# A load cut in two and a store held back: the sixth chunk of a streaming RMSNorm on one Trainium2 core

## The chip, the cores and the metric

One core of one Trainium2 chip runs the kernel. The metric is the device time of one execution in microseconds (us). The profiler takes one execution apart. Its span (first to last instruction) is about 1.8 us shorter than the measured time.

## The reference

```python
batch, seq, dim = 16, 1024, 512          # x: float32, 33.55 MB
rms = np.sqrt(np.mean(x ** 2, axis=-1, keepdims=True) + eps)
return np.maximum(x / rms * gamma, 0).astype(np.float32)
```

Every row of 512 numbers is read once and written once: 67.1 MB in all.

## The kernel before

The 16,384 rows are cut into 8 chunks of 4 MB, each with 16 rows on each of 128 partitions. SBUF holds six slots of a chunk. One queue, SyncE's (SP in the profile), carries loads and stores. ScalarE squares and sums, VectorE scales, multiplies by gamma and clips, both in place in the slot.

```python
K = 16                      # rows of a chunk on one partition
G = 8                       # rows of one step of ScalarE and VectorE
nchunks = rows // K         # 8
nslots = 6
per = K // G                # 2
...
loads = [(0, 0, G), (0, G, K - G)] + [(i, 0, K) for i in range(1, nchunks)]
...
def load(m):
    i, a, r = loads[m]
    nc.sync.dma_start(out=slot_ap(i)[:, a:a + r, :], in_=xv[i][:, a:a + r, :]
                      ).then_inc(sem_half if m == 0 else sem_slot[i % nslots], 16)
...
def store(i):
    nc.sync.dma_start(out=ov[i], in_=slot_ap(i)).then_inc(sem_slot[i % nslots], 16)
...
for m, (i, a, r) in enumerate(loads):
    if i < nslots:
        load(m)                                   # chunks 0 to 5 at once
nxt = nslots
for i in range(nchunks):
    nc.sync.wait_ge(done, per * (i + 1))          # VectorE is through with chunk i
    store(i)
    if i >= 1 and nxt < nchunks:
        nc.sync.wait_ge(sem_slot[nxt % nslots], 32)   # an old store has landed
        ...                                       # load chunk nxt into the freed slot
        nxt += 1
```

Chunks count from 0, so the sixth chunk is chunk 5. The order of the queue is: load 0 in two halves, loads 1 to 5, store 0, store 1, load 6, store 2, load 7, stores 3 to 7. The 16 DMA engines move a whole chunk as 8 packets of 32 KB each, a half chunk as 8 packets of 16 KB each. I call the transfers that are queued and not yet moved the ring; it runs dry when nothing is left in it. I call the change from a load to a store, or back, a turn. The first turn is the one from load 5 to store 0.

## Time and profile before

| what | value |
|---|---|
| time, median (range, 6 runs) | 162.84 us (162.69 to 162.93) |
| span of the profiled run | 160.9 us |
| DMA engines busy, main queue | 97.6% |
| VectorE busy, ScalarE busy | 78%, 54% |
| bytes moved, mean rate | 67.1 MB, 417 GB/s |

How to read it: all bytes go through the 16 DMA engines, which are hardly ever idle. The compute engines have breaks. The span can shrink only where the DMA engines are idle or run below their usual rate. The prediction shows the lines.

### The profile page before, as it was taken

How to read it: one execution, taken by the hardware profiler on the slowest of the kernel's cores; microseconds unless marked ns; L12 is line 12 of the kernel's file. 1: busy time of each engine (PE TensorE's matmuls, PEld its weight loads, DVE VectorE, ACT ScalarE, POOL GpSimd, SP SyncE). 2: the span in 40 equal slices, each digit the busy share in tenths (PEclk: the TensorE clock that was granted, in tenths of full speed). 3: DMA queues.
4: the chain of work that ended last, by engine and by line, in shares of the span. 5: the costliest groups of instructions: out<-in, count | busy, mean ns of one | idle time of the engine just before them, and what ended most of it. 6: DMA issues, size and time to landing. Idle time of an engine off the chain costs nothing. (4 is left out here: it accounts for less than half of the span.)

```text
span 160.9 us, 1006 instructions
## 1 busy us (share of the span) xinstructions
DVE 126.0 (78%) x164; ACT 86.3 (54%) x273; POOL 0.2 (0%) x4
## 2 busy tenths in 40 slices
DVE  1103989898989899999999999999999999994000
ACT  3088929889988988988900198503994000000000
POOL 0000000000000000000000000000000000000000
DMA  5999999999999998999999999999999999999993
GB/s 155 434 432 415 521 391 391 513 399 391 489 424 391 481 432 367 415 391 489 424 391 489 424 391 448 464 391 440 456 407 432 456 415 424 464 415 424 464 407 138
DMA packets 2456, 67.12 MB, mean 417 GB/s; under 512 B 276, under 2 KB 276, under 8 KB 280
## 3 DMA queue, kind: packets, MB, share of 16 engines
q1 hardware_dynamic: 2448, 67.11, 97.6%
q10 hardware_dynamic: 8, 0.01, 0.0%
HBM read 33.56 MB, written 33.55 MB: 417 GB/s over the span
## 5 line engine op out<-in xcount | busy, mean ns | idle before, releaser
L124 ACT ACTIVATE junk<-slots 128x512 f32 x128 | 74.5, 582 | 30.6 <-ACTq L120 30.3
L148 DVE SCALAR_TENSOR_TENSOR slots<-slots,rstd,gamma_sb 128x512 f32 x128 | 86.2, 747 | 4.8 <-DVEq L145 4.8
L155 DVE TENSOR_SCALAR slots<-slots x16 | 36.7, 2294 | 2.4 <-DVEq L154 0.2
L124 ACT ACTIVATION_READ_ACCUMULATOR junk<-slots x128 | 23.9, 187 | 0.0
L142 DVE RECIPROCAL rstd<-rms x16 | 3.1, 196 | 6.3 <-DVEq L138 6.3
L131 ACT ACTIVATE rms<-ss,eps_sb x16 | 4.8, 301 | 3.0 <-ACTq L130 3.0
L135 DVE LOAD_MASK_SELECT gamma_sb<-gseed x1 | 0.0, 14 | 5.8 <-DMA gseed<-in_gamma_dram 5.8
L116 ACT ACT_TABLE_LOAD x1 | 1.3, 1283 | 2.8 <-issue 2.8
L109 DVE MEMSET gseed<- 128x512 f32 x1 | 0.5, 485 | 1.1 <-SPq L90 1.1
L135 DVE STREAM_SHUFFLE gamma_sb<-gseed 128x512 f32<-128x512 f32 x1 | 0.7, 715 | 0.0
L180 POOL MEMSET const-bfloat16-1.0<- 128x1 bf16 x1 | 0.1, 103 | 0.0
L180 POOL MEMSET const-uint8-127<- 128x1 uint8 x1 | 0.1, 102 | 0.0
L180 POOL MEMSET const-float32-0.0<- 128x1 f32 x1 | 0.1, 100 | 0.2 <-issue 0.2
L180 POOL MEMSET const-float32-1.0<- 128x1 f32 x1 | 0.1, 99 | 0.0
L110 DVE MEMSET eps_sb<- 128x1 f32 x1 | 0.1, 59 | 0.0
## 6 DMA issues: line engine op xcount, KB each, us to landing
out_dram<-slots SPq DMA_DIRECT2D x8, 4096.0 KB, 31.3
slots<-in_x_dram SPq DMA_DIRECT2D x7, 4096.0 KB, 30.3
slots<-in_x_dram SPq DMA_DIRECT2D x2, 2048.0 KB, 9.6
gseed<-in_gamma_dram ACTq DMA_DIRECT2D x1, 8.0 KB
```

Of the source, the lines that this page charges most:

```text
L109: nc.vector.memset(gseed, 0.0).then_inc(sem_z, 1)
L110: nc.vector.memset(eps_sb, eps).then_inc(sem_z, 1)
L116: nc.scalar.preload_act_table(ACTF.Sqrt)
L124: a = nc.scalar.activation(out=junk[:, j, :], in_=slots[:, bass.ds(base + j * d, d)], func=ACTF.Square, accum_out=ss[:, bass.ds(col + j, 1)])
L131: nc.scalar.activation(out=rms[:, bass.ds(col, G)], in_=ss[:, bass.ds(col, G)], func=ACTF.Sqrt, bias=eps_sb, scale=inv_d).then_inc(sq, 1)
L135: nc.vector.stream_shuffle(gamma_sb, gseed, [0] * 32)
L142: nc.vector.reciprocal(out=rstd[:, bass.ds(col, G)], in_=rms[:, bass.ds(col, G)]).then_inc(sv, 1)
L148: r = nc.vector.scalar_tensor_tensor(out=row, in0=row, scalar=rstd[:, bass.ds(col + j, 1)], in1=gamma_sb, op0=ALU.mult, op1=ALU.mult)
L155: nc.vector.tensor_scalar_max(out=blk, in0=blk, scalar1=0.0).then_inc(done, 1)
L180: nc = _bacc.Bacc("TRN2", target_bir_lowering=False, num_devices=1)
```

## The change

The intent: the last of the initial loads comes in two pieces, so that the first store can be queued at a chosen moment, when the first piece has landed, and not stand in the queue behind three loads for 30 us.

```diff
-    loads = [(0, 0, G), (0, G, K - G)] + [(i, 0, K) for i in range(1, nchunks)]
+    loads = [(i, a, r) for i in range(nchunks)
+             for a, r in (((0, G), (G, K - G)) if i in (0, nslots - 1) else ((0, K),))]
+    sem_half2 = tc.alloc_semaphore("half2")
...
+    def piece_sem(m):
+        i, a, r = loads[m]
+        if a + r < K:
+            return sem_half if i == 0 else sem_half2
+        return sem_slot[i % nslots]
...
-                          ).then_inc(sem_half if m == 0 else sem_slot[i % nslots], 16)
+                          ).then_inc(piece_sem(m), 16)
...
         for i in range(nchunks):
             nc.sync.wait_ge(done, per * (i + 1))
+            if i == 0:
+                nc.sync.wait_ge(sem_half2, 16)
             store(i)
```

The waits for a landed load are changed to match (cut here).

More of the change, by code (lines that the diff above doesn't have):

```diff
@@ L76, in load @@
                           in_=xv[i][:, a:a + r, :]
-                          ).then_inc(sem_half if m == 0 else sem_slot[i % nslots], 16)
+                          ).then_inc(piece_sem(m), 16)
     def loaded(engine, m):
-        i = loads[m][0]
-        if m == 0:
-            engine.wait_ge(sem_half, 16)
+        i, a, r = loads[m]
+        if a + r < K:
+            engine.wait_ge(piece_sem(m), 16)
         else:
```

## The prediction

> **What bounds the kernel now.** I read the page's busy rows first, then its DMA queues, then the queue's issues in order of time, then DMA traffic in windows cut to one 4 MB transfer each. The busy rows:
>
> ```profile
> span 160.9 us, 1006 instructions
> ...
> DVE 126.0 (78%) x164; ACT 86.3 (54%) x273; POOL 0.2 (0%) x4
> ...
> q1 hardware_dynamic: 2448, 67.11, 97.6%
> ...
> HBM read 33.56 MB, written 33.55 MB: 417 GB/s over the span
> ```
>
> VectorE is 78% busy, ScalarE 54%, but the one queue that carries all of x in and all of the result out keeps the 16 DMA engines 97.6% busy. The transfers are the bound. The chain of waits says little here (it ends with VectorE at 1% of the span), since it does not follow the queue back through its earlier transfers. The queue's own issues, in order of time:
>
> ```profile
> 0.94 3.60 SPq L75 DMA_DIRECT2D slots<-in_x_dram  x7
> 31.07 16.83 SPq L87 DMA_DIRECT2D out_dram<-slots  x2
> 72.13 0.34 SPq L75 DMA_DIRECT2D slots<-in_x_dram  x1
> 72.51 0.73 SPq L87 DMA_DIRECT2D out_dram<-slots  x1
> 82.05 0.34 SPq L75 DMA_DIRECT2D slots<-in_x_dram  x1
> 82.44 64.36 SPq L87 DMA_DIRECT2D out_dram<-slots  x5
> ```
>
> The seven loads of chunks 0 to 5 are queued by 4.5 us. Stores 0 and 1 are queued at 31.08 and 47.56 us (the pair in the second row), long before the loads are through. Load 6 waits until store 0 has freed its slot, at 72.13. So store 0 was queued at 31.08 and landed at about 72.1, 41 us later, for a transfer that needs under 10 us: it stood behind loads 3, 4 and 5. The same is seen from the waits of the queue's issuer: one wait for a store, of 24.2 us, from 47.9 to 72.1. The windows, each one transfer wide (columns: window, length, busy time and count of VectorE, ScalarE, POOL, clock, DMA share, GB/s):
>
> ```profile
> 32.20:41.88 9.68, 9.23 (x14) 8.73 (x30) 0.00 (x0) 1.00 1.00 433
> 41.88:51.59 9.71, 9.26 (x13) 9.07 (x30) 0.00 (x0) 1.00 1.00 432
> 51.59:61.49 9.90, 9.45 (x13) 9.12 (x29) 0.00 (x0) 1.00 0.93 374
> 61.49:71.23 9.74, 9.14 (x12) 8.79 (x29) 0.00 (x0) 1.00 1.00 431
> 71.23:80.91 9.68, 8.94 (x13) 8.95 (x30) 0.00 (x0) 1.00 1.00 433
> 80.91:90.59 9.68, 9.23 (x13) 0.00 (x0) 0.00 (x0) 1.00 1.00 433
> 90.59:100.28 9.69, 9.24 (x13) 7.99 (x26) 0.00 (x0) 1.00 1.01 436
> ```
>
> These are load 3, load 4, load 5, store 0, store 1, load 6, store 2. Every transfer moves at 431 to 436 GB/s, except that the last of the initial loads comes out lower (374 GB/s is partly where I cut: a packet counts where it ends). The packet records tell it finely. A packet of 32 KB takes 1.213 us on its engine. The last two packets of load 5 on each engine, just before store 0, take 1.278 and 1.817 us in the mean of 16 engines, so (1.278 - 1.213) + (1.817 - 1.213) = 0.67 us are lost at the first turn from loading to storing (0.4 to 0.8 by engine in the last packet alone). No later turn costs that: the last packets of load 6 before store 2 take 1.213 us, those of load 7 before store 3 take 1.243.
>
> The rest of the span: first packet at 1.96 us, last packet's end at 159.40, last landing and end 160.9. 67.11 MB at 433 GB/s are 155.0 us, so of the 157.4 us of traffic only 2.4 are not full rate: 0.67 at the turn, 0.6 in each engine's first packet (1.204 us in the mean for a 16 KB packet, that later takes 0.611), and about 1.1 us of small packets and of the slowest engine's drift.
>
> **What the Trainium skill says.** The page "DMA: Bandwidth & Descriptors", section "Queues, rings and completion order", says that each DMA engine consumes a row's descriptors in ring order. The trace agrees: store 0's 41 us, and landings 9.7 us apart in the order of issue. The section "Anatomy of one DMA" adds that DMA engines never wait on semaphores; a wait happens in the issuing sequencer before dispatch. So a wait before a store can only cost if the ring runs dry. Its section "Where 436 GB/s comes from" puts the ceiling at 435.2 GB/s; the windows show 433, so there is no headroom in the steady stages. The page "HBM Reference", section "Specifications (TRN2)", says that a lone core streams at about 425 GB/s, bounded by its 16 DMA engines; 417 over the span and 433 in the steady stages agree. I found no page that states a cost of turning from loads to stores.
>
> **The change, part by part.**
> 1. Load 5 becomes two transfers of 8 rows: packets of 16 KB instead of 32 KB, 16 per engine instead of 8. Chunk 0 already comes so: its steady packets take 0.611 us, twice that is 1.222 against 1.213. Over 8 pairs that adds 8 x 0.009 = 0.07 us on the path. One more completion per engine is a packet of 4 bytes, of some 0.01 us. Sum: +0.08 us. The extra issue at the start (0.4 us each) comes at about 4.5 us, when load 1 has not yet begun (12.5 us): hidden.
> 2. Store 0 is queued later. In load 5 packets begin at 51.23 us. Eight packets of the first half take 8 x 0.611 = 4.9 us, so the last engine (begun 51.59) ends at 56.5. Chunk 4 landed 0.46 us after its last packet's end (52.05 against 51.59), so the first half lands at about 57.0. Store 0 is then issued in 0.34 us, and the first issue of the program took 1.02 us to its first packet (0.94 to 1.96): ready by about 58.1. The second half ends 4.9 us after the first, at 61.4. The store is in the ring 3.3 us before its turn. No gap. The chunk itself has long been computed (31.0 us), so the new wait is the only one.
> 3. Store 1 follows directly (its chunk is done at 47.5), by about 57.8 instead of 47.56. Its turn comes at 71.2. Hidden. Load 6 still waits for store 0's landing at 72.1; its turn comes at 80.9. Hidden.
> 4. Compute: ScalarE reaches chunk 5 at 69.6 us, by which time it has landed (62.4); two counts of 1 instead of one of 2 change nothing. VectorE runs on from 14.5 to 146.4 with only sub-microsecond breaks and is not touched. It is the near second: store 7 is issued at 146.46 and the ring would be dry at about 149.7, so 3.2 us minus 1.0 of issue, some 2.2 us of slack, all kept.
>
> Sum: 162.84 + 0.08 = 162.92 us if the turn's 0.67 us stays as it is.
>
> **The rivals.**
> (a) The turn is the target. With store 0 queued 26 us later, nothing of it stands in the ring while loads 3 to 5a run. If its early queueing is what stretches the last load packets, up to 0.67 us comes back (0.8 on the slowest engine): about 162.2. For it: the loss sits exactly there, and only where the store had been queued deep, behind about 25 packets per engine; store 2, queued 18 us ahead behind some 16, paid nothing. Against: the new store is still 3.3 us, some five 16 KB packets, ahead of its turn; and packets did not get slower when store 0 was queued at 31 us (1.213 before and after). I give it one chance in five.
> (b) The turn's loss belongs to the first write of the output, as the first read has 0.6 us extra in its first packet: then it stays, at the same 0.6 to 0.7 us whatever is queued when. 162.9. This is what I think likeliest, though nothing in the trace shows the cause.
> (c) The new wait runs late and leaves the ring empty: it would take 3.3 us more than I worked out. A wait that then adds x us makes the time 162.9 + x. The landings of half chunks scatter by 0.35 us between engines, so I give this under 5%.
> (d) Smaller packets at the turn: with 16 KB packets the engines drift apart differently, and the loss may be a little smaller or larger, 0.2 us either way.
>
> **The range and the chances.** Even the best case, the whole 0.67 us back and all else free, is 0.4% of 162.84; even removing all 2.4 us that are not full rate would be 1.5%. So 2% faster is out of reach for a change that moves no fewer bytes, and 2% slower needs a gap of 3.3 us in the ring beyond the 3.3 us of margin. The weights: 0.75 on 162.9 and 0.2 on 162.2, the rest above; the middle is 162.8. The range adds the spread of the three runs of before (162.69 to 162.90): 162.1 to 163.3. Chances: faster 0.01, same 0.98, slower 0.01.
>
> **What would show it.** In the changed profile: eight issues of loads up to about 5 us; two stores issued together at about 57 us in place of 31.08 and 47.56; load 6 still issued at about 72; packets of load 5 of 16 KB at about 0.611 us; the window of store 0 still beginning at about 61.5; VectorE ending within 0.3 us of 146.4. Rival (a) is right if the last packets before store 0 are within 0.05 us of their usual length and everything after comes about 0.6 us sooner. Rival (c) is right if the records show a stretch of idle engines between the second half of chunk 5 and store 0. I am wrong altogether if the times move by more than 1 us without either.

## The result, and the profile after

| | before | after |
|---|---|---|
| median of 6 runs | 162.84 us | 162.75 us |
| range | 162.69 to 162.93 | 162.67 to 162.91 |

The ratio is 0.9996, with a 95% interval of 0.9983 to 1.0009: the same. A ratio is the mean time of one kernel's runs over that of the other's of the same rounds, so not quite the ratio of the medians quoted.

Span and main queue, from the page of the changed kernel:

```profile
span 160.9 us, 1009 instructions
...
q1 hardware_dynamic: 2592, 67.11, 97.6%
```

Three more instructions and 144 more packets (128 data packets, since 16 per engine replace 8, and 16 completions), but the same bytes, the same share of busy DMA engines, the same span. (The busy times of VectorE and ScalarE and the mean rate are the same to the last digit too.) The queue's issues in order of time, changed kernel (columns: start, length, queue, line, operation, tensors, count; a merged row runs from its first issue's start to its last issue's end):

```profile
0.94 4.14 SPq L84 DMA_DIRECT2D slots<-in_x_dram  x8
57.10 0.82 SPq L96 DMA_DIRECT2D out_dram<-slots  x2
72.13 0.34 SPq L84 DMA_DIRECT2D slots<-in_x_dram  x1
72.51 0.96 SPq L96 DMA_DIRECT2D out_dram<-slots  x1
82.04 0.34 SPq L84 DMA_DIRECT2D slots<-in_x_dram  x1
82.42 64.43 SPq L96 DMA_DIRECT2D out_dram<-slots  x5
```

The new wait did its work: stores 0 and 1 are queued at 57.10 and 57.49 us. Before the change they were queued at 31.08 and 47.56. Yet load 6, which waits for store 0's landing, goes out at 72.13 us in both kernels. The 26 us of delay vanished within the queue: the store's turn had not come.

For the turns I cut windows from the first packet of each transfer to the first packet of the next. The length of the window (second column) is then what the transfer took, and GB/s must fit it. Here are load 4, load 5 and store 0, before:

```profile
41.52:51.22 9.70, 9.25 (x13) 9.23 (x30) 0.00 (x0) 1.00 1.00 432
51.22:61.48 10.26, 9.81 (x14) 9.31 (x31) 0.00 (x0) 1.00 1.01 409
61.48:71.22 9.74, 9.14 (x12) 8.79 (x29) 0.00 (x0) 1.00 1.00 431
```

And after:

```profile
41.49:51.19 9.70, 9.25 (x13) 9.22 (x30) 0.00 (x0) 1.00 1.00 432
51.19:61.46 10.27, 9.82 (x14) 9.32 (x31) 0.00 (x0) 1.00 1.02 408
61.46:71.14 9.68, 9.09 (x12) 8.73 (x29) 0.00 (x0) 1.00 1.00 433
```

The one slow transfer is the same in both: load 5, 10.26 and 10.27 us where 9.68 to 9.70 is usual (9.74 for store 0 before). The price of the first turn did not move.

One refinement serves the experiments. The window's edge is the first of the 16 engines to begin. Taking the mean of the 16 first-packet starts instead, from the packet records, gives a step per transfer that no single engine sways. The usual step is 9.69 us. What a step has over that I call its excess. It is a mean over the engines, while the time follows the engine that ends last, so excesses need not add up to the change in time. Load 5's excess is 0.70 us before and 0.73 after.

### The profile page after: what moved, and what is told of

It is laid out like the page before. It is cut to its first block, busy times and chain, and to the rows that moved or that the text cites. A ratio compares the mean times of both kernels' runs of the same rounds, so it can differ in the third digit from the quotient of the medians.

```text
span 160.9 us, 1009 instructions
## 1 busy us (share of the span) xinstructions
DVE 126.0 (78%) x164; ACT 86.3 (54%) x273; POOL 0.2 (0%) x4
```

## The experiments

All kernels gave correct results. Kernels of one call ran on one chip beside the kernel before. Its medians there were 162.74, 162.78 and 162.74 us. This table holds the excess of each transfer in us, from one profiled execution each (blank: 0.03 or less):

| kernel | time, median | ratio to before | load 5 | store 0 | store 1 | load 6 | later, or elsewhere |
|---|---|---|---|---|---|---|---|
| before | 162.84 | | 0.70 | | | | |
| after | 162.75 | 0.9996 | 0.73 | | | 0.06 | |
| split alone | 162.62 | 0.9992 | 0.54 | | | 0.11 | |
| tiny early store | 162.88 | 1.0009 | 0.80 | | | | |
| store 0 after load 3 | 163.13 | 1.0020 | | | | | load 3: 1.13 |
| pieces 12 + 4 | 163.21 | 1.0030 | 0.09 | | 0.23 | 0.87 | |
| pieces 14 + 2 | 164.08 | 1.0077 | 0.56 (gap) | 0.08 | 0.79 | 1.05 | |
| wait for the whole load | 165.31 | 1.0160 | 1.65 (gap) | 0.08 | 0.77 | 1.14 | |
| emptied before store 2 | 165.66 | 1.0182 | 0.69 | | | 1.65 (gap) | store 2: 0.84, load 7: 1.03 |
| emptied before store 3 | 163.98 | 1.0076 | 0.81 | | | | load 7: 1.70 (gap), stores 3 to 6: 0.03 to 0.08 |
| extra bytes, 8 engines | 164.11 | 1.0077 | | | | 0.43 | load 0: 1.67 above before; store 6: 0.16 |
| extra bytes, 16 engines | 164.88 | 1.0124 | | | | | load 0: 2.40 above before |

(Load 0 has an excess of its own at the start of every run, 0.73 us before; it is left out but for the last two rows.) "Gap" means that the engines were idle between the two transfers; elsewhere they were busy and packets took longer.

My theory at the outset: the ring of queued transfers is the bound, neither part of the change touches it, and the 0.7 us at the first turn belongs to the first write of the output. The rivals: the two parts cancel; the long queueing of store 0 causes the 0.7 us; a long run of loads causes it.

### 1. The split without the wait

```diff
-            if i == 0:
-                nc.sync.wait_ge(sem_half2, 16)
             store(i)
```

(against the changed kernel)

> The changed kernel without the new wait: load 5 in two halves, store 0 queued at 31 us again. Theory (neither part touches the bound): 162.8, the turn costs 0.6 to 0.7 us as with the wait, VectorE ends at 146.4. Rival 'the two parts work against each other, the split costs and the late queueing gains': the split alone would be slower than the kernel before by over 0.2 us, with packets of load 5 over 0.62 us each.

Measured: 162.62 us (4 runs, 162.53 to 162.69), ratio 0.9992 (0.9976 to 1.0007). Store 0 was queued at 31.18 us. Load 5's packets of 16 KB took 0.612 to 0.616 us in the mean until the turn. The windows of load 5 and store 0:

```profile
51.20:61.31 10.11, 9.66 (x14) 9.16 (x31) 0.00 (x0) 1.00 1.02 415
61.31:70.99 9.68, 9.08 (x12) 8.73 (x29) 0.00 (x0) 1.00 1.00 433
```

The split costs nothing that can be told from noise, and so the wait gains nothing that the split would hide. The excess, 0.54 us, is a little below the expected 0.6 to 0.7. The kernels that are identical to the one before up to this turn show 0.69 to 0.81 in single executions, so I read nothing into that. Whether the split alone gains a tenth of a per cent is open: its interval includes 1.

### 2. Store 0 waits for all of load 5

```diff
+            if i == 0:
+                nc.sync.wait_ge(sem_slot[nslots - 1], 16)
             store(i)
```

(against the kernel before, as in all that follow but the two with pieces)

> The kernel before with store 0 waiting for all of load 5 (landed at about 62.2 us), load 5 in one piece. Theory 'a wait before a store costs only what it leaves the ring dry': issue at 62.2, first packet 1.0 us later at 63.2 against 61.5, so 1.5 to 1.9 us of idle engines between load 5 and store 0 and about 164.2 in all (some 0.6 us less if the turn's stretched packets vanish: 163.7). Rival 'the issue latency overlaps, the ring refills at once': under 0.4 us, 163.0.

Measured: 165.31 us (165.11 to 165.44), ratio 1.0160 (1.0145 to 1.0176). Store 0 was issued at 61.76 us. The windows of load 5, store 0, store 1 and load 6:

```profile
51.15:62.60 11.45, 10.86 (x15) 10.50 (x35) 0.00 (x0) 1.00 0.85 366
62.60:72.37 9.77, 9.23 (x12) 8.82 (x29) 0.00 (x0) 1.00 1.00 429
72.37:82.58 10.21, 9.56 (x13) 7.75 (x26) 0.00 (x0) 1.00 1.03 411
82.58:93.45 10.87, 10.42 (x15) 0.00 (x0) 0.00 (x0) 1.00 1.00 386
```

The gap is as expected: a DMA share of 0.85 in load 5's window, first packet 0.85 us after the issue's start, 1.65 us of excess with no stretched packet. But the time rose by 2.57 us, over a microsecond more than I expected. The rest is in the third and fourth windows: the turns at the end of store 1 and of load 6, free in the kernel before, now cost 0.77 and 1.14 us. Both my theory and the rival missed this.

### 3. A tiny store ahead of the first turn

```diff
+        nc.vector.memset(warm, 0.0).then_inc(sem_z, 1)
...
+        nc.scalar.wait_ge(sem_z, 3)
+        nc.scalar.dma_start(out=ov[0][:, 0, 0:128], in_=warm).then_inc(sem_w, 16)
...
+            if i == 0:
+                nc.sync.wait_ge(sem_w, 16)
             store(i)
```

> The kernel before, plus one tiny store (128 rows of 512 bytes of zeros into the first output rows, overwritten later by store 0, which waits for it) issued at about 3 us on the other queue. Theory 'first write of the output': the last load packets before store 0 are back at 1.21 us each (they took 1.28 and 1.82 in the mean before, 0.67 us lost), the time falls by up to 0.6 us to about 162.2, less what the tiny store costs at the start (0.15 us by its bytes). Rival 'the turn from a long run of loads costs 0.67 us whatever came before': the turn stays at 0.6 to 0.7 us and the time is 162.8 to 163.0.

Measured: 162.88 us (5 runs, 162.74 to 163.17), ratio 1.0009 (0.9995 to 1.0023). Load 5's window:

```profile
51.37:61.61 10.24, 9.79 (x14) 9.29 (x31) 0.00 (x0) 1.00 1.03 410
```

The excess at the turn is 0.80 us although 512 bytes in each of store 0's 128 stretches of output had been written long before. (That store was issued at 2.77 us; its packets ran from 6.4 to 11.5 us.) So "the first write of the output" is not the reason, as far as a touch of that size can show it. The 128 small store packets ran in between packets of load 0, which still took 0.611 us each: that an engine changes between loading and storing was not dear by itself there.

### 4. The first store turned earlier

```diff
-            if i < nslots:
+            if i < nslots - 2:
                 load(m)
...
             store(i)
+            if i == 0:
+                load(nslots - 1)      # chunk 4
+                load(nslots)          # chunk 5
```

> The kernel before with loads 4 and 5 queued only after store 0, so that store 0 turns the ring at about 41.9 us, after three fewer... that is after load 3, and load 5 is followed by store 1 at about 71 us, a second turn after two loads in a row. Theory 'first turn': the 0.6 to 0.7 us sit before store 0 at 41.9, and the turn at 71 us costs under 0.1. Rival 'a long run of loads': both turns cost, the second perhaps less. Rival 'depth of queueing' (store 0 is queued 11 us, about nine packets per engine, ahead here, against 25 packets in the kernel before): no cost at 41.9. Time 162.7 to 163.0 by the first theory, since nothing else is moved.

Measured: 163.13 us (162.93 to 163.18), ratio 1.0020 (1.0004 to 1.0035). Load 3 (now before store 0) and, further down, load 5 (now before store 1):

```profile
31.66:42.42 10.76, 10.31 (x15) 9.81 (x32) 0.00 (x0) 1.00 1.01 390
...
61.78:71.46 9.68, 9.23 (x11) 7.89 (x26) 0.00 (x0) 1.00 1.00 433
```

The first turn pays here too, after four loads in place of six (1.13 us, more than expected), and the turn after two loads in a row is free. A long run of loads is not needed for a dear turn: in experiment 2 the turn after load 6 alone cost 1.14 us. (Experiment 6 will show that it is not enough either.) And the store was queued only about nine packets per engine ahead, not 25, and its turn cost more, not less: deep queueing is not the cause. (What happens when the store is queued just before its turn is for experiment 7.)

What was left? In experiment 2, where later turns became dear, the 16 engines began store 0 within 0.14 us of each other; in the kernel before they began load 5 within 0.36 us, paid, and ran 0.5 us or more apart afterwards, without paying again. So I formed a new theory, called lockstep below: a turn is dear when all engines reach it together. Its rival: only the first turns of a run are dear, as a kind of warm-up.

### 5. The ring emptied in mid-run

```diff
+            if i == 2:
+                nc.sync.wait_ge(sem_slot[0], 48)      # load 6 has landed
             store(i)
```

> The kernel before, but store 2 waits for load 6 to have landed (about 91.4), which empties the ring once in mid-run and makes the engines start store 2 together. Theory 'lockstep' (a turn costs where the 16 engines reach it within about 0.4 us of each other, as at the first turn, and not where they are spread by 0.5 us or more): the gap of 1.4 to 1.8 us, the spread of the starts drops from 0.5 to under 0.2 us, and the next turns (store 2 to load 7, load 7 to store 3) cost 0.5 to 1.0 us each where they cost 0.0 before: 165.0 in all, between 164.8 and 165.6. Rival 'only the first two or three turns of a run cost, warm-up of whatever kind': the gap alone, 164.2 to 164.6, later turns 0.0 to 0.1.

Measured: 165.66 us (165.50 to 165.88), ratio 1.0182 (1.0165 to 1.0199). Load 6, store 2, load 7:

```profile
80.72:92.37 11.65, 11.04 (x15) 0.67 (x3) 0.00 (x0) 1.00 0.83 360
92.37:102.68 10.31, 9.87 (x14) 9.78 (x33) 0.00 (x0) 1.00 1.02 407
102.68:113.43 10.75, 10.15 (x13) 0.30 (x1) 0.00 (x0) 1.00 1.00 390
```

A gap of 1.65 us, then two dear turns of 0.84 and 1.03, though the run's earlier turns (0.69, then two free ones) were behind it. The warm-up rival falls. The engines started store 2 within 0.15 us of each other (0.62 at the start of load 6), as the lockstep theory had it.

### 6. Spreading the engines, and the control

```diff
+    lag = singles.tile([8, 5 * d], F32, name="lag")       # control: [16, 5 * d]
...
+        nc.scalar.dma_start(out=lag.rearrange("p (k d) -> p k d", d=d),
+                            in_=xv[0][0:8, 0:5, :]).then_inc(sem_w, 16)   # control: 0:16
...
+            if i == 0:
+                nc.sync.wait_ge(sem_w, 16)
             store(i)
```

> The kernel before, plus one 80 KB load into a scratch tile on 8 of the 16 engines at the start (10 KB each), so that these engines run about 0.38 us behind the others and the engines reach the first turn spread by about 0.75 us in place of 0.36. Theory 'lockstep': the turn's stretch falls from 0.67 us to under 0.25 in the mean, time 162.4 to 162.9 (0.38 us of bytes added on the late engines, up to 0.6 saved). Rival 'a fixed price of the first turn': 0.6 to 0.7 us still, time 163.1 to 163.3.

> Control of the staggered run: the same 10 KB on each of the 16 engines, no stagger. Both theories: spread about 0.4 us at the first turn, 0.6 to 0.7 us lost there, time 163.1 to 163.3 (162.8 plus 0.38 by its bytes). If its turn is also cheap, the spread is not what matters in the staggered run.

Measured: 164.11 us (163.84 to 164.66), ratio 1.0077 (1.0060 to 1.0093), and 164.88 us for the control (164.49 to 164.98), ratio 1.0124 (1.0106 to 1.0143). The packet records show 8 and 16 packets of 10 KB, as meant. Load 5's window, first of the spread run, then of the control:

```profile
52.71:62.41 9.70, 9.25 (x14) 8.75 (x29) 0.00 (x0) 1.00 1.00 432
```

```profile
53.57:63.28 9.71, 9.26 (x13) 8.76 (x29) 0.00 (x0) 1.00 1.00 432
```

The first turn is free in both, after six loads in a row. So the control speaks against the lockstep reading: its engines were not staggered on purpose and began load 5 within 0.49 us of each other (1.51 us in the spread run). As 0.49 us lies at the edge of what the theory calls together, the control alone does not refute it. Both runs paid at the start instead: the packets beginning at 6 to 10 us took 1.36 and 1.44 us per engine more than usual, and load 0 took 1.67 and 2.40 us more than in the kernel before, for 0.38 us of bytes on an engine (the first of these packets took 0.385 us). The spread run also paid 0.43 us at the end of load 6. The extra transfer differs from the loads in more than its bytes: it comes on a second queue and lands in only 8 or 16 partitions. Which of these made the start dear, and why the first turn was then free, no run separates. The times missed every expectation. (In the spread run the compute began later too and store 7 was issued only at 149.30 us, which the 0.16 us of store 6 may reflect.)

### 7. How late may the store be queued?

```diff
-    ... (((0, G), (G, K - G)) if i in (0, nslots - 1) else ((0, K),))]
+    ... (((0, G), (G, K - G)) if i == 0 else
+         ((0, 14), (14, 2)) if i == nslots - 1 else ((0, K),))]     # and (0, 12), (12, 4)
...
-            nc.gpsimd.sem_inc(ready, r // G)
+            nc.gpsimd.sem_inc(ready, per if r == K else 1)
```

(against the changed kernel)

> The changed kernel with load 5 cut 14 and 2 rows, store 0 queued once the 14 have landed (estimate: last packet's end 60.4, landing and issue 60.6 to 60.9, first packet possible 0.85 us after the issue as in the run that waited for the whole load, so 61.5 to 61.8 against the second piece's end at 61.2 to 61.5). Theory 'only a dry ring costs': 0 to 0.5 us of gap, 162.7 to 163.3, between the changed kernel and the run with the whole wait (165.3). Rival 'the order to wait is itself the cost of the whole-wait run (its 2.6 us)': over 164.5.

Measured with 14 + 2 rows: 164.08 us (163.89 to 164.16), ratio 1.0077 (1.0060 to 1.0094); issue at 60.82 us, store 0's first packet at 61.65. The last packets of load 5 had ended at 61.16 to 61.44, so the gap was small (0.2 to 0.6 us by engine), as expected. The time was not: 0.8 us above the upper end.

> The changed kernel with load 5 cut 12 and 4 rows: the 12 have landed and store 0 is queued at about 59.4 to 59.6 us, its first packet possible 0.85 us later, 60.3 to 60.5, against the end of load 5 at 61.5. Theory 'only a dry ring costs': no gap, the turn's stretch of 0.6 to 0.75 us as ever, 162.6 to 163.0. Rival 'a store queued only some 1 us ahead no longer stretches the last load packets': stretch under 0.2 us, 162.2. Rival 'the ring needs more lead than 1 us': a gap of 0.1 to 0.5 us and about 164.

Measured with 12 + 4 rows: 163.21 us (162.75, 162.99, 163.42, 163.47), ratio 1.0030 (1.0003 to 1.0058); issue at 59.44 us. Load 5 to load 6:

```profile
51.13:60.92 9.79, 9.34 (x14) 8.84 (x29) 0.00 (x0) 1.00 1.01 429
60.92:70.68 9.76, 9.16 (x12) 8.81 (x29) 0.00 (x0) 1.00 1.00 432
70.68:80.52 9.84, 9.39 (x12) 9.20 (x31) 0.00 (x0) 1.00 1.01 426
80.52:91.03 10.51, 9.77 (x14) 0.30 (x1) 0.00 (x0) 1.00 1.00 396
```

This is the most telling run. There is no gap, and the price of the first turn is all but gone: 429 GB/s in load 5's window, an excess of 0.09 us. The rival that expected this is right on the turn and wrong on the time, since store 1 and load 6 pay 0.23 and 0.87 us. The excesses from load 5 to load 6 sum to 1.21 us, against 0.70 before. Queueing the store just in time saved nothing; turns that were free became dear. One rival stands untested: the last packets before the turn are 8 KB here, and no run has these pieces without the wait, so the packet size may have a part in it. (With 16 KB packets, in experiment 1, the price stayed at 0.54 us.)

### 8. The ring emptied where no turn follows

```diff
+            if i == 3:
+                nc.sync.wait_ge(sem_slot[1], 48)      # load 7 has landed
             store(i)
```

> The kernel before, but store 3 waits for load 7 to have landed (about 111.1 us), which empties the ring where only stores follow, so no turn comes after it. Theory 'the gap costs its own length and the turns after it cost extra': gap of 1.4 to 1.8 us and nothing else, less what the closer ends of the engines give back (they ended 1.03 us apart before): 163.7 to 164.6. Rival 'an emptied ring costs 2.6 to 2.9 us whatever follows' (the size of the two runs that emptied it ahead of turns): 165.3 to 165.7.

Measured: 163.98 us (163.81 to 164.03), ratio 1.0076 (1.0058 to 1.0093). Load 7 and store 3:

```profile
100.15:111.91 11.76, 11.17 (x15) 3.41 (x12) 0.00 (x0) 1.00 0.83 357
111.91:121.68 9.77, 9.32 (x12) 9.29 (x32) 0.00 (x0) 1.00 1.00 429
```

The gap is as long as in experiment 5 (1.70 and 1.65 us), but the time rises by 1.24 us, not 2.88. It is less than the gap because the engines ended within 0.18 us of each other and not 1.03: the mean of their ends came 1.96 us later, the last end only 1.38 us. So an emptied ring costs about its gap, less what the closer ends give back; what came on top elsewhere belongs to the turns that followed it.

**What stands.** In ten of the twelve kernels a price of 0.5 us or more is paid at a turn; the two of experiment 6 paid over 1 us at the start, before any turn, and then nothing at the first one (0.43 us at the end of load 6 in one of them). In the five kernels that paid at the first turn and kept the ring full throughout, later turns were free or nearly so (up to 0.11 us); after a just-in-time store or an emptied ring, the next two turns pay. That much is shown. The mechanism is not. The first write (for a touch of 512 bytes), the length of the load run and deep queueing (beyond the 3.5 us ahead of the changed kernel) are excluded as causes; how closely the engines run together does not explain the dear turns at the end of load 6 in experiment 2 and of load 7 in experiment 5, whose engines had begun those loads 0.65 and 0.61 us apart, and hardly the control. Each excess is from one execution. I know of no run here that avoids every such price, and no kernel here clearly beats the one before.

## Why the prediction was right

- **The bound.** Predicted: the transfers, and a wait costs only if the ring runs dry. The result fits: store 0 was queued 26 us later, and the time did not move. The trace agrees that the wait sits in the issuer: SyncE's wait before store 0, 51.9 us long, ended when the half load had landed at 57.0 us, and the engines went on meanwhile. (The section that the prediction names for this is headed as the one for transfers issued from GpSimd; and the steady 433 GB/s are 2% above the 425 that it says agree.) Experiments 2 and 8 show the wait's cost once the ring does run dry. The premise is incomplete, though: the 12 + 4 run never ran dry and still was 0.3% slower.
- **The split.** Predicted +0.08 us. The halves' packets took 0.612 to 0.616 us in the mean (0.611 assumed). Load 5's excess rose by 0.03, within what single executions vary. The split alone was not slower. Too small to be measured, as the sum had it.
- **The late store.** Predicted: landing at about 57.0 us, store ready by 58.1, in the ring 3.3 us before its turn. Measured: issue at 57.10, store 0's first packet at 61.47. The first packet can follow 0.83 to 0.85 us after the issue's start (experiments 2, 5, 7, 8), not 1.02, so the margin was about 3.5 us.
- **Store 1, load 6, compute.** Store 1 was issued at 57.49 us, load 6 at 72.13, ScalarE began chunk 5 at 69.64, VectorE ended at 146.49 (146.43 before). All hidden, as predicted.
- **Rival (a), 0.67 us back at one chance in five.** It did not happen: 0.73 us of excess. Its reason, a store queued deep, fails here and in experiment 4, for stores still some packets ahead. In experiment 7 a far later store (with smaller packets) did empty the first turn of its price, and the next two turns paid.
- **Rival (b), the price stays.** It did, but the reason I thought likeliest, the first write of the output, is refuted for a 512-byte touch by experiment 3. Here the forecast was right and its explanation was not, so that part was luck.
- **Rival (c), a gap.** None in the changed kernel. Experiment 7 places the edge: issue at 57.10 us is free, 59.44 costs 0.3%, 60.82 costs 0.8%, and experiment 2's 61.76 costs 1.6%.
- **The ceiling.** The most that the change could win back, 0.67 us or 0.4%, and the margin of over 3 us before the wait could cost were what made "within 2%" near certain, whatever the cause of the price.

## What to carry to other kernels

With one in-order queue that kept the DMA engines 97% busy, the moment at which store 0 was queued was worth nothing between 30 and 3.5 us ahead of its turn; 0.6 us ahead, with smaller pieces, already cost 0.3%. Find a transfer's turn from the landings before judging a wait. When an edit removes a visible stretch of slow packets, look at the following turns before counting a gain, since the loss may only have moved. Give an experiment that adds something a control that adds the same without the effect: the control here put in doubt a theory that two runs had seemed to confirm.

## What the Trainium skill lacked or had wrong

- "DMA: Bandwidth & Descriptors" states no cost of turning a full ring from loads to stores. In five kernels that kept their ring full the first turn cost 0.54 to 1.13 us, and later ones next to nothing (up to 0.11 us). It is no fixed price: in three others with a full ring the first turn cost 0.09 us or less, and in two of these later ones cost up to 0.87 us.
- The same page says nothing of what follows an emptied ring. Besides the gap (1.65 to 1.70 us when the issuer waits for the landing of the transfer before), the next two turns cost 0.77 to 1.14 us each; without a turn after it, only the gap and up to 0.08 us a store are paid.
- The same page gives about 0.6 us to the first byte of a transfer issued from SyncE ("Latency and other measured facts"). The runs show 0.83 to 0.85 us from the issue's start to the first packet on an empty ring, of which 0.33 to 0.34 is the issue itself. The page's line does not say where it counts from: for the issue's start it is too low, for its end (about 0.5 us) too high.
